# Binary cross-entropy, one core: the last chunk's clip placed earlier, the last chunk computed in four equal pieces

## The chip, the cores and the metric

The kernel runs on one core of one Trainium2 chip. The metric is the device time in microseconds (us) of one execution. A profiled execution gives a trace of every instruction, of the packets that the core's 16 DMA engines move, and of semaphore increments.

## The reference

Two inputs of 8192 x 8192 float32 and one output of that size.

```
eps = 1e-7
pred = np.clip(pred, eps, 1 - eps)
return -(target * np.log(pred) + (1 - target) * np.log(1 - pred))
```

The targets are 0 or 1, so the result is -ln|pred + target - 1|. The kernel computes that.

## The kernel before

The 67 million elements are cut into n = 64 chunks of 128 partitions x 8192 columns. Two rings of four slots hold pred (float32) and target (converted to bf16 by its load). Everything is computed in place in the pred ring. The order in the program is the order on each engine.

```python
    def load(k):
        queue = nc.sync if k == 0 else nc.gpsimd
        queue.dma_start(out=slot(ring_p, k), in_=pred_c[k])
        nc.gpsimd.dma_start(out=slot(ring_t, k), in_=target_c[k])

    def store(k, off=0, w=W):
        queue = nc.sync if k >= n - 2 else nc.gpsimd
        queue.dma_start(out=out_c[k, :, off : off + w], in_=slot(ring_p, k, off, w))

    def clip(k, off=0, w=W):        # VectorE: max, min
        ...
    def front(k, off=0, w=W):       # VectorE: t - 1 + p, then ScalarE: Abs, Ln
        ...
    def back(k, off=0, w=W):        # VectorE: times -1
        ...
    # (cut: the first chunk)
        for k in range(1, n - 1):
            clip(k)
            front(k)
            back(k - 1)
            store(k - 1)

            if k >= 2 and k - 2 + SLOTS < n:
                load(k - 2 + SLOTS)
        back(n - 2)
        store(n - 2)

        h, q = W // 2, W // 4
        clip(n - 1)
        front(n - 1, 0, h)
        front(n - 1, h, q)
        back(n - 1, 0, h)
        store(n - 1, 0, h)
        front(n - 1, h + q, q)
        back(n - 1, h, q)
        back(n - 1, h + q, q)
        store(n - 1, h, h)
```

I call the last two stores, of 2 MB each, half 1 and half 2.

Of the kernel before, what the change touches and what calls it, by code (L numbers as in the profile page):

```python
# [1 line left out]

# [4 lines left out]

EPS = 1e-7



W = 8192
SLOTS = 4



@with_exitstack
def kernel(
    ctx: ExitStack,
    tc: tile.TileContext,  # L20
    pred: bass.AP,
    target: bass.AP,
    out: bass.AP,
):






    nc = tc.nc
    fp32 = mybir.dt.float32
    bf16 = mybir.dt.bfloat16
    Alu = mybir.AluOpType
    Act = mybir.ActivationFunctionType
    P = nc.NUM_PARTITIONS

    R, C = pred.shape
    n = R * C // (P * W)
    assert n * P * W == R * C and n > SLOTS  # L40

    def chunks(ap):
        return ap.rearrange("r c -> (r c)").rearrange("(k p w) -> k p w", p=P, w=W)

    pred_c, target_c, out_c = chunks(pred), chunks(target), chunks(out)

    pool = ctx.enter_context(tc.tile_pool(name="rings", bufs=1))
    ring_p = pool.tile([P, SLOTS * W], fp32, name="ring_p", tag="ring_p")
    ring_t = pool.tile([P, SLOTS * W], bf16, name="ring_t", tag="ring_t")
    warm = pool.tile([1, 8], fp32, name="warm", tag="warm")  # L50

    def slot(ring, k, off=0, w=W):
        c = k % SLOTS * W + off
        return ring[:, c : c + w]
# [10 lines that stand above are left out]
    def clip(k, off=0, w=W):  # L65
        p = slot(ring_p, k, off, w)
        nc.vector.tensor_scalar(  # L67
            out=p, in0=p, scalar1=EPS, scalar2=1 - EPS, op0=Alu.max, op1=Alu.min
        )

    def front(k, off=0, w=W):
        p, t = slot(ring_p, k, off, w), slot(ring_t, k, off, w)
        nc.vector.scalar_tensor_tensor(  # L73
            out=p, in0=t, scalar=1.0, in1=p, op0=Alu.subtract, op1=Alu.add
        )
        nc.scalar.activation(out=p, in_=p, func=Act.Abs)  # L76
        nc.scalar.activation(out=p, in_=p, func=Act.Ln)  # L77

    def back(k, off=0, w=W):
        p = slot(ring_p, k, off, w)  # L80
        nc.vector.tensor_scalar(out=p, in0=p, scalar1=-1.0, scalar2=None, op0=Alu.mult)  # L81

    with tc.manual_schedule():
        for k in range(SLOTS):
            load(k)
        nc.vector.memset(warm, 1.0)  # L86
        nc.scalar.activation(out=warm, in_=warm, func=Act.Ln)  # L87
        clip(0)
        front(0)
# [5 lines that stand above are left out]

            if k >= 2 and k - 2 + SLOTS < n:
                load(k - 2 + SLOTS)
        back(n - 2)
        store(n - 2)

        h, q = W // 2, W // 4
        clip(n - 1)
        front(n - 1, 0, h)
        front(n - 1, h, q)
        back(n - 1, 0, h)
        store(n - 1, 0, h)
        front(n - 1, h + q, q)
        back(n - 1, h, q)
        back(n - 1, h + q, q)
        store(n - 1, h, h)  # L110


# [1 line left out]
_INS = ['pred', 'target']  # L114
_OUTS = [((8192, 8192), 'float32')]


# [23 lines left out]
```

## Time and profile before

| | before |
|---|---|
| time, median of the first 3 runs | 1871.18 us (1870.36 to 1873.4) |
| profiled span | 1869.4 us |
| busy: DVE (VectorE), ACT (ScalarE) | 60%, 48% |
| DMA, mean of the 16 engines | 9 tenths or more in 39 of 40 slices |

From the page of the kernel before: busy time by engine, then the DMA engines' busy share in tenths for 40 equal slices of the span, then the two queues that carry the data (packets, MB, share of 16 engines' span).

```profile
DVE 1117.4 (60%) x197; ACT 902.2 (48%) x134; POOL 110.6 (6%) x193
...
DMA  9999999999999999999999999999999999999998
...
q0 software_dynamic: 27216, 658.52, 98.8%
q1 hardware_dynamic: 576, 12.58, 1.6%
```

The kernel is bound by its bytes: the DMA engines are at least 90% busy in every slice but the last. Queue q0 is the one that GpSimd issues on, q1 the one that SyncE (SP) issues on. A rearrangement of compute can help only where a DMA engine stands still, and the slices leave room for that mainly at the end.

The timeline of the kernel before, tail only. Columns: start in us, duration, engine, source line, operation, output<-input, count, and in brackets the idle time before it and who ended that. L67 is the clip, L73 the first operation of front, L76 Abs, L77 Ln, L81 the negation (back), L63 the stores.

```profile
1824.64 7.03 ACT L77 ACTIVATE ring_p<-ring_p 128x8192 f32<-128x8192 f32 x1
1831.70 4.43 DVE L81 TENSOR_SCALAR ring_p<-ring_p 128x8192 f32<-128x8192 f32 x1 [9.82 <-ACT ring_p L77]
1836.05 4.42 DVE L67 TENSOR_SCALAR ring_p<-ring_p 128x8192 f32<-128x8192 f32 x1
1836.16 26.10 SPq L63 DMA_DIRECT2D out_dram<-ring_p  x3
1840.50 6.63 DVE L73 SCALAR_TENSOR_TENSOR ring_p<-ring_t,ring_p 128x4096 f32<-128x4096 bf16 x2
1844.96 3.62 ACT L76 ACTIVATE ring_p<-ring_p 128x4096 f32<-128x4096 f32 x1 [13.29 <-DVE ring_p L73]
...
1860.67 1.23 DVE L81 TENSOR_SCALAR ring_p<-ring_p 128x2048 f32<-128x2048 f32 x1 [2.78 <-ACT ring_p L77]
```

DVE waits 9.82 us for the Ln of chunk n-2, only then negates, then clips the last chunk. ACT meanwhile waits 13.29 us. That idle stretch is what the change goes for. The merged SP line covers three stores: the first is issued at 1836.16 and the last, half 2, about 0.34 us (one issue) before 1862.26, so at 1861.9.

The windows view of the kernel before, for the same tail. Columns: stretch, its length, busy time of DVE, ACT and POOL, clock, busy share of the DMA engines, GB/s.

```profile
1848.00:1852.00 4.00, 0.00 (x0) 3.97 (x2) 0.00 (x0) 1.00 1.04 451
1852.00:1856.00 4.00, 3.74 (x2) 3.93 (x3) 0.00 (x0) 1.00 0.45 193
1856.00:1860.00 4.00, 1.89 (x2) 3.18 (x2) 0.00 (x0) 1.00 1.05 446
1860.00:1863.00 3.00, 1.23 (x1) 0.64 (x1) 0.00 (x0) 1.00 0.26 109
1863.00:1868.30 5.30, 0.00 (x0) 0.00 (x0) 0.00 (x0) 1.00 0.82 346
```

Here are the two holes in the DMA work: 0.45 busy from 1852 to 1856 and 0.26 from 1860 to 1863. But a mean over 16 engines does not say whether the engine that finishes last had a hole. The trace's landing records are needed. Each transfer raises its semaphore sixteen times, once by each DMA engine that has finished its share, so sixteen times come from one transfer (the Trainium skill, "DMA: Bandwidth & Descriptors", section "Why a DMA increments its semaphore by 16 and not by 1", says that the engines finish independently; the spreads below agree). Kernel before, first and last of the sixteen:

```
                              first     last
target of chunk n-2          1804.54   1808.76
pred of chunk n-1            1823.93   1828.15
target of chunk n-1          1833.59   1837.81
store of chunk n-3           1846.92   1856.00
store of chunk n-2           1852.98   1857.22
half 1                       1860.67   1862.07
half 2                       1868.03   1868.23
```

One engine is 4.2 us behind the first at the loads, and so is its end of store n-2. (The increments name no engine; that the last one is the same each time is read from the equal distances.) I call that distance the lag. After store n-2 the last engine went straight on to half 1 (4.85 us, eight packets of 0.61 us). Its hole came only then: by the packet records its last packet of half 1 ended at 1861.73, 0.34 us before the increment, and the first packets of half 2 started, on the sixteen engines, at 1862.75 to 1862.90. So the last engine stood still for 1.0 to 1.2 us.

The chain of waits that ended last, kernel before (start, duration, what), ends like this:

```profile
1852.26 2.29 DVE ring_p L81
1854.55 2.21 DVE ring_p L73
1856.76 0.02 issue
1856.79 1.92 ACT ring_p L76
1858.70 0.02 issue
1858.73 1.92 ACT ring_p L77
1860.65 0.02 issue
1860.67 1.23 DVE ring_p L81
```

Its last piece is the negation that releases half 2, at 1861.9.

The page's list of DMA issues (size of each, median time from issue to landing) has for the two halves:

```profile
out_dram<-ring_p SPq DMA_DIRECT2D x2, 2048.0 KB, 6.9
```

### The profile page before, as it was taken

The numbers are of one execution on the slowest core, as the hardware profiler recorded it, in microseconds if no ns is written. First come the engines' busy times: TensorE is split into PE (matmuls) and PEld (weight loads), VectorE is DVE, ScalarE is ACT, GpSimd is POOL, SyncE is SP. The second block draws the span as 40 slices with busy tenths as digits, with TensorE's granted clock in tenths as the row PEclk, the third lists the DMA queues.
The fourth block names the chain that finished last, engine by engine and source line by source line (L and its number), as shares of the span: only waits on it lengthen the run. The fifth ranks groups of instructions, "written<-read, shape, count | busy, mean of one in ns | idle before, by whom it ended". The sixth has DMA issues, their size and how long they took to land.

```text
span 1869.4 us, 755 instructions
## 1 busy us (share of the span) xinstructions
DVE 1117.4 (60%) x197; ACT 902.2 (48%) x134; POOL 110.6 (6%) x193
## 2 busy tenths in 40 slices
DVE  4946564666656656566565665656656666566564
ACT  3643644536355364453544535445354463553645
POOL 0210000000000000000000000000000000000000
DMA  9999999999999999999999999999999999999998
GB/s 325 337 377 352 351 376 344 376 353 350 381 344 373 358 347 385 344 368 364 346 384 346 361 370 344 382 350 355 375 345 378 353 351 381 345 372 358 347 385 330
DMA packets 27797, 671.14 MB, mean 359 GB/s; under 512 B 3088, under 2 KB 3088, under 8 KB 3088
## 3 DMA queue, kind: packets, MB, share of 16 engines
q0 software_dynamic: 27216, 658.52, 98.8%
q1 hardware_dynamic: 576, 12.58, 1.6%
q14 instruction: 5, 0.04, 0.0%
HBM read 536.87 MB, written 268.44 MB: 431 GB/s over the span
## 4 chain that ended last, share of the span: by engine, by line
issue 86%; DMA 6%; POOL 5%; DVE 2%; ACT 1%; POOLq 0%; DVEq 0%; PEldq 0%
DMA ring_t<-in_target_dram 4%; DMA out_dram<-ring_p 2%; POOL ring_t L59 2%; POOL out_dram L63 2%; POOL ring_p L58 1%; DVE ring_p L73 1%; ACT ring_p L76 1%; ACT ring_p L77 1%; DVE ring_p L81 1%; DVE ring_p L67 0%; POOLq L58 0%; DVEq L73 0%; PEldq L136 0%; POOLq L63 0%
## 5 line engine op out<-in xcount | busy, mean ns | idle before, releaser
L76 ACT ACTIVATE ring_p<-ring_p 128x8192 f32<-128x8192 f32 (+1 forms) x66 | 450.4, 6824 | 955.6 <-DVE ring_p L73 955.6
L73 DVE SCALAR_TENSOR_TENSOR ring_p<-ring_t,ring_p 128x8192 f32<-128x8192 bf16 (+1 forms) x66 | 556.5, 8433 | 325.1 <-DMA ring_t<-in_target_dram 325.0
L67 DVE TENSOR_SCALAR ring_p<-ring_p 128x8192 f32<-128x8192 f32 x64 | 283.3, 4426 | 400.9 <-DMA ring_p<-in_pred_dram 400.9
L77 ACT ACTIVATE ring_p<-ring_p 128x8192 f32<-128x8192 f32 (+1 forms) x66 | 450.4, 6824 | 2.1
L81 DVE TENSOR_SCALAR ring_p<-ring_p 128x8192 f32<-128x8192 f32 (+1 forms) x66 | 283.1, 4290 | 17.7 <-ACT ring_p L77 17.7
L63 POOL DMA_DIRECT2D out_dram<-ring_p x62 | 40.8, 658 | 1692.7 <-DVE ring_p L81 1662.7
L58 POOL DMA_DIRECT2D ring_p<-in_pred_dram x63 | 36.1, 573 | 18.4 <-DMA out_dram<-ring_p 18.1
L59 POOL DMA_DIRECT2D ring_t<-in_target_dram x64 | 35.3, 552 | 0.8 <-PEq L136 0.8
L87 ACT ACT_TABLE_LOAD x1 | 1.3, 1283 | 0.7 <-PEq L125 0.7
L86 DVE MEMSET warm<- 1x8 f32 x1 | 0.1, 65 | 0.8 <-PEq L125 0.8
L87 ACT ACTIVATE warm<-warm 1x8 f32<-1x8 f32 x1 | 0.2, 207 | 0.0
L125 POOL MEMSET const-float32-0.0<- 128x1 f32 x1 | 0.1, 99 | 0.2 <-issue 0.2
L125 POOL MEMSET const-bfloat16-1.0<- 128x1 bf16 x1 | 0.1, 102 | 0.0
L125 POOL MEMSET const-float32-1.0<- 128x1 f32 x1 | 0.1, 99 | 0.0
L125 POOL MEMSET const-uint8-127<- 128x1 uint8 x1 | 0.1, 99 | 0.0
## 6 DMA issues: line engine op xcount, KB each, us to landing
ring_p<-in_pred_dram POOLq DMA_DIRECT2D x63, 4096.0 KB, 34.5
out_dram<-ring_p POOLq DMA_DIRECT2D x62, 4096.0 KB, 25.3
ring_t<-in_target_dram POOLq DMA_DIRECT2D x64, 2048.0 KB, 43.6
ring_p<-in_pred_dram SPq DMA_DIRECT2D x1, 4096.0 KB, 19.6
out_dram<-ring_p SPq DMA_DIRECT2D x1, 4096.0 KB, 21.1
out_dram<-ring_p SPq DMA_DIRECT2D x2, 2048.0 KB, 6.9
```

Of the source, the lines that this page charges most:

```text
L58: queue.dma_start(out=slot(ring_p, k), in_=pred_c[k])
L59: nc.gpsimd.dma_start(out=slot(ring_t, k), in_=target_c[k])
L63: queue.dma_start(out=out_c[k, :, off : off + w], in_=slot(ring_p, k, off, w))
L67: nc.vector.tensor_scalar(out=p, in0=p, scalar1=EPS, scalar2=1 - EPS, op0=Alu.max, op1=Alu.min)
L73: nc.vector.scalar_tensor_tensor(out=p, in0=t, scalar=1.0, in1=p, op0=Alu.subtract, op1=Alu.add)
L76: nc.scalar.activation(out=p, in_=p, func=Act.Abs)
L77: nc.scalar.activation(out=p, in_=p, func=Act.Ln)
L81: nc.vector.tensor_scalar(out=p, in0=p, scalar1=-1.0, scalar2=None, op0=Alu.mult)
L86: nc.vector.memset(warm, 1.0)
L87: nc.scalar.activation(out=warm, in_=warm, func=Act.Ln)
L125: nc = _bacc.Bacc("TRN2", target_bir_lowering=False, num_devices=1)
```

## The change

The intent is to use DVE's idle 9.82 us for the last chunk's clip, so that its front can start as soon as its target is there, and to hand ACT its first piece after 2048 columns rather than 4096. The stores stay two halves.

```diff
             if k >= 2 and k - 2 + SLOTS < n:
                 load(k - 2 + SLOTS)
+        clip(n - 1)
         back(n - 2)
         store(n - 2)
 
-        h, q = W // 2, W // 4
-        clip(n - 1)
-        front(n - 1, 0, h)
-        front(n - 1, h, q)
-        back(n - 1, 0, h)
-        store(n - 1, 0, h)
-        front(n - 1, h + q, q)
-        back(n - 1, h, q)
-        back(n - 1, h + q, q)
-        store(n - 1, h, h)
+        q = W // 4
+        front(n - 1, 0, q)
+        front(n - 1, q, q)
+        front(n - 1, 2 * q, q)
+        back(n - 1, 0, q)
+        back(n - 1, q, q)
+        store(n - 1, 0, 2 * q)
+        front(n - 1, 3 * q, q)
+        back(n - 1, 2 * q, q)
+        back(n - 1, 3 * q, q)
+        store(n - 1, 2 * q, 2 * q)
```

## The prediction

> **What bounds the kernel.** The DMA engines: the page's slice table has DMA at 9 tenths or more in all slices but the last; DVE is busy 60%, ACT 48%. The loop is untouched, so only the tail after about 1828 us of the 1869.4 us span can change.
>
> **What the change does.** DVE's clip (4.43 us) moves; the front is cut in four pieces of 2048 (2.28 us each) instead of 4096 + 2048 + 2048. ACT gets two more instructions (1.92 us a piece, 3.62 us at 4096). The stores stay two of 2 MB.
>
> By the timeline and the trace's landing records:
> - Before: DVE idles 9.82 us until the Ln of chunk n-2 ends (1831.68). Then negation to 1836.1, clip to 1840.5, front of 4096 to 1844.9, ACT, half stores issued at 1854.55 and 1861.9.
> - The last pred landed at 1828.15, the last target at 1837.81. So the clip now runs 1828.2 to 1832.6 in that gap, the negation to 1837.05 (its store 0.9 us later), and the fronts begin at 1837.9, held by the target: 2.6 us earlier.
> - The first piece reaches ACT at 1840.2, not 1844.96. Eight activations of about 1.93 us: to 1855.7. Negation 1.22 us.
> - Half stores are issued at about 1849.15 and 1856.9, 5.4 and 5.0 us earlier.
>
> **Why most of that is not saved.** The DMA engines have a backlog. In the trace each store's sixteen semaphore increments give one time per engine. Store n-2 was done on the first engine at 1852.98, on the last at 1857.22: one engine runs 4.2 us behind, as at earlier loads. The Trainium skill, "DMA: Bandwidth & Descriptors", section "Why a DMA increments its semaphore by 16 and not by 1", says that engines finish independently and the semaphore counts them; this trace agrees, with that spread. Half 1, issued at 1854.55, ended at 1860.7 on most engines but at 1862.07 on the last, 4.85 us (eight 16 KB packets of 0.61 us) after its previous store. The lagging engine never waited for half 1; issuing that earlier does nothing for it. It idled only from 1862.07 until half 2 reached it, about 1863.1; half 2 ended at 1868.03 to 1868.23.
>
> After: half 2 is queued at 1856.9, before the lagging engine ends half 1 at about 1862.0; it follows directly and ends at about 1862.0 + 4.9 = 1866.9. The other engines end it near 1863.2. So of 5.0 us of earlier issue about 1.3 us is saved.
>
> **Predicted time:** 1871.2 - 1.3, about 1869.8 us, range 1866.5 to 1872.2 (the runs before spread 3 us, more than the gain). Without the lag the saving would be 5 us. Chances: faster by over 2% 0.005, within 2% 0.99, slower 0.005.
>
> **What would show each step right or wrong.**
> - Timeline: clip at 1828.2 inside the old gap; first front at 1837.9 on the target; last negation ends near 1856.9.
> - Issues: half stores' time to landing grows from 6.9 us (median) to 10 to 13 us.
> - Landing records: half 1's last engine still at about 1862.0; half 2's first near 1863, last near 1866.9. If half 2 ends on all engines by 1863.5, the lag theory is wrong and 5 us is saved.
> - Span about 1868.1 us.
>
> **What would make it wrong.** A lag that differs from run to run; two queues sharing an engine otherwise with more stores queued; the later store n-2 leaving engines idle.

## The result, and the profile after

| | before | after |
|---|---|---|
| median of 4 runs each | 1871.44 us | 1869.59 us |
| lowest to highest | 1870.36 to 1873.4 | 1869.04 to 1870.06 |
| ratio, 95% interval | | 0.9989 (0.9972 to 1.0006) |
| profiled span | 1869.4 us | 1867.5 us |
| lag in the profiled run | 4.2 us | 3.65 us |

A ratio is the mean time of one kernel's fast runs over that of the other's of the same rounds, so it is not quite the ratio of the medians. The whole interval lies within 2% of 1. It also includes 1, so the times alone show no gain.

Timeline of the changed kernel, the same tail:

```profile
1827.61 4.43 DVE L67 TENSOR_SCALAR ring_p<-ring_p 128x8192 f32<-128x8192 f32 x1 [6.32 <-DMA ring_p<-in_pred_dram]
1831.95 4.42 DVE L81 TENSOR_SCALAR ring_p<-ring_p 128x8192 f32<-128x8192 f32 x1
1836.40 19.96 SPq L63 DMA_DIRECT2D out_dram<-ring_p  x3
1837.34 6.69 DVE L73 SCALAR_TENSOR_TENSOR ring_p<-ring_t,ring_p 128x2048 f32<-128x2048 bf16 x3 [0.97 <-DMA ring_t<-in_target_dram]
1839.66 1.91 ACT L76 ACTIVATE ring_p<-ring_p 128x2048 f32<-128x2048 f32 x1 [8.58 <-DVE ring_p L73]
1841.61 1.91 ACT L77 ACTIVATE ring_p<-ring_p 128x2048 f32<-128x2048 f32 x1
1843.42 1.90 ACT L76 ACTIVATE ring_p<-ring_p 128x2048 f32<-128x2048 f32 x1
...
1854.77 1.23 DVE L81 TENSOR_SCALAR ring_p<-ring_p 128x2048 f32<-128x2048 f32 x1 [2.52 <-ACT ring_p L77]
```

The schedule does what it was meant to: the clip runs as soon as pred lands, the front waits for the target (the bracket names its load), and ACT starts 5.3 us earlier. Half 2 is issued at 1856.0 instead of 1861.9. Windows of the changed kernel, same stretches:

```profile
1848.00:1852.00 4.00, 3.69 (x3) 3.97 (x3) 0.00 (x0) 1.00 1.01 434
1852.00:1856.00 4.00, 1.48 (x2) 2.71 (x2) 0.00 (x0) 1.00 0.94 401
1856.00:1860.00 4.00, 0.00 (x0) 0.00 (x0) 0.00 (x0) 1.00 1.00 430
1860.00:1863.00 3.00, 0.00 (x0) 0.00 (x0) 0.00 (x0) 1.00 0.85 366
1863.00:1868.30 5.30, 0.00 (x0) 0.00 (x0) 0.00 (x0) 1.00 0.10 43
```

Both holes are closed; what follows after 1863 is a few engines finishing late. The landing records show it engine by engine:

```
                              first     last
target of chunk n-2          1804.52   1808.17
target of chunk n-1          1833.56   1837.24
store of chunk n-2           1852.94   1856.63
half 1                       1857.81   1861.48
half 2                       1862.66   1866.35
```

The first engine ends 5.4 us earlier than before (1862.66 for 1868.03), the last only 1.9 us (1866.35 for 1868.23), and the last one counts. The halves now wait in the queue, which the issue list shows as a longer time to landing:

```profile
out_dram<-ring_p SPq DMA_DIRECT2D x2, 2048.0 KB, 11.6
```

The lag differs between the two runs, and both ends move with it. A measure free of that is the distance D from the last engine's landing of target n-2 (the load that releases the tail's compute) to the last engine's landing of half 2. Before: 1868.23 - 1808.76 = 59.47 us. After: 1866.35 - 1808.17 = 58.18 us. The change is worth 1.29 us; the other 0.6 us of the 1.9 us is the smaller lag (3.65 for 4.2) of that run.

### The profile page after: what moved, and what is told of

Same layout as the page of the kernel before. It is cut to its first block, busy times and chain, and to the rows that moved or that the text cites. A ratio compares the mean times of both kernels' runs of the same rounds, so it can differ in the third digit from the quotient of the medians.

```text
span 1867.5 us, 759 instructions
## 1 busy us (share of the span) xinstructions
DVE 1117.6 (60%) x199; ACT 902.4 (48%) x136; POOL 110.6 (6%) x193
## 4 chain that ended last, share of the span: by engine, by line
issue 87%; DMA 6%; POOL 5%; DVE 1%; ACT 1%; POOLq 0%; DVEq 0%; PEldq 0%
DMA ring_t<-in_target_dram 4%; DMA out_dram<-ring_p 2%; POOL ring_t L59 2%; POOL out_dram L63 2%; POOL ring_p L58 1%; DVE ring_p L73 1%; ACT ring_p L77 0%; ACT ring_p L76 0%; DVE ring_p L81 0%; POOLq L58 0%; DVEq L73 0%; PEldq L138 0%; POOLq L63 0%
```

## The experiments

My theory, "backlog": the last DMA engine has the bytes of the stores ahead of it still to move when the halves are issued, and a store that is issued before it runs dry gains nothing. The rival, "compute chain": the chain that the profile shows as ending last sets the end, so 5 us earlier at the issue is worth about 5 us. Issue times below are taken, like D, from the last engine's landing of target n-2.

| run | lag | half 2 issued | D |
|---|---|---|---|
| before | 4.2 | 53.2 | 59.47 |
| after | 3.65 | 47.9 | 58.18 |
| after, again | 7.2 | 47.8 | 58.18 |
| clip moved alone | 3.9 | 50.6 | 58.21 |
| four pieces alone | 4.0 | 50.4 | 58.20 |
| after, last Ln left out | 4.0 | 43.6 | 58.18 |
| after, last chunk in one store | 5.5 | 47.9 (all) | 58.96 |
| before, no store of n-2 | 2.8 | 53.2 | 59.42 |
| after, no store of n-2 | 4.0 | 47.9 | 54.13 |
| before, 8 chunks | 0.9 | 53.2 | 59.45 |
| after, 8 chunks | 1.9 | 48.3 | 58.62 |

### The clip alone

```diff
@@ against the kernel before
+        clip(n - 1)
         back(n - 2)
         store(n - 2)
 
         h, q = W // 2, W // 4
-        clip(n - 1)
         front(n - 1, 0, h)
```

> Clip moved ahead of the negation, pieces left at 4096 + 2048 + 2048. Read as the distance D from the last engine's landing of target n-2 to the last engine's landing of half 2 (before 59.47 us, after 58.18 us), which takes out the run's own lag. Half 1 should be issued about 2.5 us later than in the changed kernel and half 2 about 2.7 us later (near 1858.7 against 1856.0 in the changed kernel's time). Backlog theory: both halves still reach the lagging engine before it has run out of work, so D stays at 58.2 +- 0.2 and the time is that of the changed kernel. Compute-chain rival: the last issue sets the end, so D is about 60.9 less what half 2 gains by finding idle engines, above 59. Time in rounds within 0.2% of before under both.

Measured: half 2 was issued at 50.6, which is 2.75 us later than in the changed kernel, and D was 58.21. Time 1870.18 us against 1870.73 us, ratio 0.9993 (0.9977 to 1.001). In the timeline of this run the front again waits for the target, and the last negation starts 20.17 us after that front, where the changed kernel's took 17.43 us (1837.34 to 1854.77):

```profile
1839.42 6.63 DVE L73 SCALAR_TENSOR_TENSOR ring_p<-ring_t,ring_p 128x4096 f32<-128x4096 bf16 x2 [0.97 <-DMA ring_t<-in_target_dram]
...
1859.59 1.23 DVE L81 TENSOR_SCALAR ring_p<-ring_p 128x2048 f32<-128x2048 f32 x1 [2.78 <-ACT ring_p L77]
```

Those 2.75 us of compute cost nothing. The rival falls.

### The four pieces alone

```diff
@@ against the kernel after
-        clip(n - 1)
         back(n - 2)
         store(n - 2)
+        clip(n - 1)
```

> Four pieces of 2048, clip left behind the negation. Half 1 near 1850.9 and half 2 near 1858.5 in the changed kernel's time, 2.5 us later than there. Backlog theory: D 58.2 +- 0.2, as with the whole change, so the two parts are not additive: each alone gives the whole 1.3 us. Compute-chain rival: D about 2.5 us above the changed kernel's, 60.7, or at least clearly above 58.2.

Measured: half 2 issued at 50.4, D 58.20; 1869.64 us against 1870.73 us, ratio 0.9993 (0.9978 to 1.0008). Measured by D, either part alone gives the whole gain; together they give no more.

### Much less compute

```diff
@@ against the kernel after
-        nc.scalar.activation(out=p, in_=p, func=Act.Ln)
+        if k < n - 1:
+            nc.scalar.activation(out=p, in_=p, func=Act.Ln)
```

> The changed kernel with the Ln of the last chunk left out: wrong on purpose in the last chunk. ACT has four activations fewer there, about 7.5 us, so half 2 is issued near 1848.5 rather than 1856.0. Backlog theory: D 58.2 +- 0.2, no gain at all from 7.5 us of compute. Compute-chain rival: D falls by several us, towards 51 to 53.

Measured: the result is wrong, as meant. Half 2 was issued 4.3 us earlier than in the changed kernel, not 7.5: with ACT shorter, the fourth front, which stands behind two negations on DVE, became what ACT waited for. That part of the expectation was a miss. D was 58.18, the same to 0.01 us, and the halves only stood longer in the queue:

```profile
out_dram<-ring_p SPq DMA_DIRECT2D x2, 2048.0 KB, 14.9
```

### Taking the backlog away

In both kernels the store of chunk n-2 is left out, so 4 MB less stand in front of the halves.

```diff
@@ against the kernel before, and against the kernel after
         back(n - 2)
-        store(n - 2)
```

> The kernel before without the store of chunk n-2: wrong on purpose in that chunk, 4 MB of writes less in front of the last two stores. Its last engine was idle ahead of half 2 anyway, so what was queued before does not matter. Backlog theory: the half stores are issued as before and half 2 ends 6.3 us after its issue; D stays at 59.5 +- 0.3.

> The changed kernel without the store of chunk n-2, the same 4 MB less. The last engine ends the store of chunk n-3 about 38.8 us after the landing of target n-2, just before half 1 is issued, so nothing stands in front of either half. Backlog theory: half 1 takes about 6.2 us, half 2 is issued at about 47.8 us and ends 6.3 us later, D = 54.1 +- 0.4; against the other kernel without that store the change now saves 5.4 us, four times 1.3. If the saving stays at 1.3 us (D 58.2), the backlog is not what holds it back.

Measured: D 59.42 for the kernel before, 54.13 for the changed one. Without the backlog the same edit is worth 5.29 us, its full gain in issue time; with it, 1.29 us. The windows of the changed kernel without that store show the DMA engines at 0.47 and 0.77 where they were at 1.01 and 0.94 with it, so now they wait for the halves:

```profile
1848.00:1852.00 4.00, 3.53 (x3) 3.97 (x4) 0.00 (x0) 1.00 0.47 197
1852.00:1856.00 4.00, 1.49 (x2) 3.58 (x2) 0.00 (x0) 1.00 0.77 328
```

and each half takes its bare time from issue to landing:

```profile
out_dram<-ring_p SPq DMA_DIRECT2D x2, 2048.0 KB, 6.3
```

This is the test that separates cause from coincidence: only the bytes in front were removed, and the lost 4 us came back. It empties SyncE's queue as well as removing bytes, so on its own it doesn't tell the order in a queue from the bytes; that it is the bytes rests on the sum of packet times further below (29.18 us for 29.11 measured).

### Does it take a lagging engine?

The prediction said that without the lag the saving would be 5 us. The lag builds up over the first chunks, so a run over 8 of 64 chunks has little of it.

```diff
@@ against the kernel before, and against the kernel after
-    assert n * P * W == R * C and n > SLOTS
+    n = 8
```

> The kernel before, run over the first 8 chunks of 64: wrong on purpose in the rest. The lag between engines builds up over the first 500 us (0.5 us at the start, 1.2 us at 227 us, 4.2 us from 1200 us on), so here it should be about 1 us at the tail. D should be 59.5 +- 0.3 whatever the lag, because the whole chain hangs on the last engine's landing of target n-2.

> The changed kernel over the first 8 chunks, lag about 1 to 2 us. My prediction said that without the lag the saving would be 5 us: that would be D near 54.5 at no lag and about 55.5 at a lag of 1. Backlog theory in its plain form: every engine, first or last, has the store of chunk n-2 and half 1 still queued when half 2 comes, so the lag plays no part in the difference, D = 58.2 +- 0.3 and the saving against the short kernel before is again 1.3 us.

Measured, at lags of 0.9 and 1.9 us: D 59.45 before and 58.62 after. The saving is 0.8 us and not 5, so that sentence of the prediction is wrong. The second value is 0.4 us above the full kernel's and slightly outside what I expected. The lag was still growing there: the last engine's landings of targets n-2 and n-1 are 29.51 us apart, where they are 29.07 us apart in the full kernel. From target n-1 on, the changed kernel needs 29.11 us in both, 1866.35 - 1837.24 and 238.75 - 209.64. The spans themselves (239.0 before, 239.6 after) even go the other way: a single run's lag hides a gain of this size.

### Two halves or one store

```diff
@@ against the kernel after
         back(n - 1, 0, q)
         back(n - 1, q, q)
-        store(n - 1, 0, 2 * q)
         front(n - 1, 3 * q, q)
         back(n - 1, 2 * q, q)
         back(n - 1, 3 * q, q)
-        store(n - 1, 2 * q, 2 * q)
+        store(n - 1)
```

> The changed kernel with the last chunk stored in one 4 MB transfer after its last negation, issued where half 2 is now, 47.8 us after the last engine's landing of target n-2. That engine ends the store of chunk n-2 at 48.5 us; the transfer reaches it 1.25 us after issue and takes 9.7 us (eight packets of 1.21 us). Backlog theory: D = 58.8 +- 0.2, only 0.6 us more than with two halves. Rival (splitting the store is what gains): half 2 alone takes 6.3 us after its issue where engines are free, a whole chunk 11, so splitting should be worth some 4.7 us and D should rise by that.

Measured: D 58.96, 0.8 us more than with two halves, where the rival expected 4.7. The time was 1872.9 us (1870.67 to 1874.24) against 1870.83, ratio 1.001 (0.9995 to 1.0026); the medians differ more than D does, with lags in the untraced runs that I can't see. With the backlog in front, splitting the last store matters little. In this run all engines ended together (1868.54 to 1868.69), 11.1 us after the issue: the first packets started 0.83 to 0.98 us after it, where I had put 1.25. So here the issue, not the backlog, set the end. With nothing in front, by these traces, the split would be worth about 4.8 us (an estimate: 11.1 less the 6.3 us of half 2).

### The changed kernel again

No edit.

> The changed kernel unaltered, for a tighter interval and a second trace. Backlog theory: 1.3 us saved, ratio 0.9993, give or take the lag of each run (3 to 4.5 us seen so far, nothing to do with the change), so medians between 0.5 and 2.5 us apart; D 58.2 again. Compute-chain rival: 5 us or more, ratio 0.997.

Measured over 5 rounds: 1870.28 us (1868.5 to 1872.84) against 1870.83 us of 9 runs, ratio 0.9996 (0.9983 to 1.0008). The profiled run had a lag of 7.2 us and a span of 1871.0 us, 3.5 us longer than the first profile of the same program, whose lag was 3.5 us smaller. D was 58.18 again. So the scatter of these times goes with the lag, and five rounds cannot settle 1.3 us. Taking all that were run, 9 times of the changed kernel have a mean of 1869.9 us and 21 of the kernel before 1871.1 us, on several chips; that agrees with 1.3 us but is no verdict.

### Moving bytes off the last engine

Three attempts at a version that beats both kernels by working on the lag itself. None did. In the first the last store leaves one DMA engine out for most of its rows:

```diff
@@ against the kernel after
-        store(n - 1, 2 * q, 2 * q)
+        p = slot(ring_p, n - 1, 2 * q, 2 * q)
+        d = out_c[n - 1, :, 2 * q : 4 * q]
+        nc.sync.dma_start(out=d[0:120], in_=p[0:120])
+        nc.sync.dma_start(out=d[120:128], in_=p[120:128])
```

> The changed kernel with half 2 stored as two transfers, partitions 0 to 119 and 120 to 127. If the first uses 15 engines and the second 8, the increments tell which engine lags: 15 times in the first. If the engine left out by the first is the one that is last, the first transfer's last increment comes near 3.1 us behind its first, not 3.7, and D is 58.2 or a little less. If the last engine is in the second transfer's eight, D grows by one 16 KB packet, 0.6 us, to 58.8. Backlog theory in both: the end is the last engine's bytes after its previous store at 26.9 GB/s, nothing else.

Measured: D = 1870.40 - 1809.84 = 60.56, 2.4 us worse, and 1873.43 us in its one run. I expected 0.6 us worse at most. The increments confirm 15 engines for the first transfer (one at once, fifteen later) and 8 for the second. But the 16 KB packets, 0.61 us in every half store before, now took up to 1.88 us, so the arrival order no longer tells which engine lags. Why they slow down is open.

In the other two, more transfers go through SyncE's queue.

```diff
@@ against the kernel after: all stores on SyncE
     def store(k, off=0, w=W):
-        queue = nc.sync if k >= n - 2 else nc.gpsimd
+        queue = nc.sync
@@ in another kernel: all pred loads on SyncE
     def load(k):
-        queue = nc.sync if k == 0 else nc.gpsimd
+        queue = nc.sync
```

> The changed kernel with all stores on the SyncE queue instead of the GpSimd queue; loads as they were. An exploration of what is left: the lag between engines. If the GpSimd queue's transfers make the engines drift apart, the lag at the tail should be smaller than 3 to 4.5 us and the time lower by up to 3 us. If not, the steady period of 29.06 us a chunk (its bytes at the engines' rate) keeps the time within 3 us of the changed kernel's.

> The changed kernel with all pred loads on the SyncE queue, target loads and stores on GpSimd's. The same exploration from the other side: a smaller lag and up to 3 us less if the GpSimd queue causes the drift; within 3 us of the changed kernel if not. [...]target loads, which now wait behind less, should land earlier against pred loads.

Measured: stores on SyncE 1876.21 us, ratio 1.0028 (1.0014 to 1.0041), clear of 1 on the slow side; pred loads on SyncE 1871.96 us, ratio 1.0005 (0.9991 to 1.0019). The first is 5.9 us above the changed kernel of the same session (1870.28), so the 3 us that I expected was a miss; the second is within them. The last engine ended the store of chunk n-2 3.45 and 4.0 us after the first, against 3.7 in the changed kernel, and the last increment of the last target load came 7.1 and 4.2 us after the first, against 3.7, so the lag was not clearly smaller. With the stores on SyncE the last target came 10 us later (1847.69 for 1837.24) and half 2 ended on all engines together, 6.3 us after its issue: there the compute chain does set the end. The same holds with the pred loads on SyncE (1868.28, for an issue at 1862.00). There the last target landed 15.5 us after the last pred (1839.09 for 1823.59), in the changed kernel 9.7 us, so "earlier against pred loads" was a miss too. The target loads stayed on the GpSimd queue in both, so these runs don't say whether that queue has a part in the lag.

## Why the prediction was right, and where not

- **DMA-bound, only the tail can change.** Right: the steady part ran alike in both (the first engine's landing of target n-1 at 1833.59 and 1833.56).
- **The schedule.** Right: clip on pred's landing, front on the target's, half 2 issued 5.3 us earlier relative to the target of n-2 (predicted 5.0). ACT's spacing was mis-sized at 1.93 us for each activation. The trace has 1.95 from an Abs to the Ln that needs it and 1.81 from a Ln to the next, independent Abs. The Trainium skill, "ScalarE: Activation LUTs", section "What ACT_TABLE_LOAD costs", says "Back-to-back ACTIVATEs overlap by ≈ 93 ns"; the 1.91 us instruction followed after 1.81 agrees. The dependent pair, at 1.95 us, shows no such overlap. The wrong size cost nothing, as the issue had slack.
- **About 1.3 us of 5 us is saved.** Right: D fell by 1.29 us. In both kernels the last engine ended half 1 at 53.31 us after target n-2 (1862.07 - 1808.76 and 1861.48 - 1808.17). By the packet records its last packet of half 1 ended at 52.97 before (1861.73 - 1808.76), and the first packets of a half start about 0.85 us after its issue. So half 2 had to be issued by about 52.1 to follow without a hole. Before, it was issued at 53.2, about 1.0 us too late; now, at 47.9, it has 4.3 us to spare. The hole of 1.0 to 1.2 us is nearly all of the 1.29 us. That the median of the first four runs, 1869.59 us, came so close to the predicted 1869.8 is luck: the same kernel scattered from 1868.5 to 1872.84 us later.
- **Why.** Right about the backlog, though not about the part of the lag in it (next point): taking away the 4 MB in front brought back the rest (5.29 us), and 4.3 us less or 2.75 us more of compute changed nothing. From the landing of target n-1 on, the changed kernel's last engine is never idle: stores n-3 and n-2 are 16 packets of 1.213 us and the halves 16 of 0.611, together 29.18 us (an estimate from the trace's packet times), and 29.11 us were measured.
- **"Without the lag the saving would be 5 us."** Wrong. With a lag of 1 to 2 us the saving was 0.8 us. No run had no lag at all. Every engine, first or last, has the same bytes to move in the tail (in the changed kernel the first took 29.10 us from target n-1 to half 2, 1833.56 to 1862.66, the last 29.11), and less lag starts the compute chain earlier by as much as it starts the last engine's work. The lag picks which engine is last; the backlog is what holds the gain back.
- **A lag that differs from run to run** was named as a risk. It came true, 2.8 to 7.2 us among the traces of full-length runs with the queues as they were, and spans go with it, so the timed ratio can't resolve the gain. What causes the lag is open; slow packets while it grew are told in the list below.

## What to carry to other kernels

When a compute chain ends in a store, ask when the last DMA engine would run out of earlier work: a store that is issued early enough for its first packets to be there by then (here about 0.85 us before) is early enough, and issuing it earlier still was worth nothing here. The chain of waits shows the compute and not that deadline; the sixteen increments of each transfer do. And for an effect of a tenth of a per cent, measure a distance inside one trace, between two events that share the run's own drift, before trusting medians.

## What the Trainium skill lacked or had wrong

- "DMA: Bandwidth & Descriptors", section "Latency and other measured facts": it says that two of the sixteen engines are usually slower, by a cause it calls a best guess. In the kernel before four engines were 2.9 us or more behind at the last loads, in the changed kernel three by more than 2 us. In the tail before the halves no engine was slower per packet: every 32 KB data packet took 1.21 to 1.23 us. The lag was an offset that grew from 0.5 us in the first loads to 3.5 us at 420 us and 4.2 us at 1200 us in the kernel before, then stayed; another run of the changed kernel reached 7.2 us. While it grew there were slow packets. From 60 to 500 us, 105 of 1920 packets of the target loads took over 1.25 us (up to 1.95, where 1.23 is usual), 26 us too long in sum over all engines. From 500 us to 1790 us none did, and the lag grew by 0.3 us. In the run that reached 7.2 us, 58 more came after 500 us. The records name no engine, so it is not shown that these packets fell on the engines that lag. No page describes the lag as such an offset.
- Same page and section: it gives about 600 ns to the first byte for a transfer issued from SyncE, without saying from when it counts. With nothing queued on most engines, half 2's first packets started 0.83 us or more after its issuing instruction began (1862.75 for 1861.92), which is 0.50 us after that instruction ended (1862.25), so no contradiction is shown. Its landing came 6.3 us after issue.
- Same page, section "Why a DMA increments its semaphore by 16 and not by 1": what it says of the engine count held (15 for 120 partitions, 8 for 8). That section gives no figure for what such a shape can cost: here 16 KB packets of up to 1.88 us instead of 0.61, from a cause that is open.
- No page that I found gives the idea that a store has a deadline set by the backlog in front of it: 5.3 us of earlier issue were worth 1.29 us with 4 MB more in front and 5.29 us without.
